# Feed-forward gate-up pairs of four feature tiles at a time, tokens stationary and 512 weight columns moving

## The chip, the cores and the metric

The kernel runs on one core of one Trainium2 chip. The metric is the device time of one execution in microseconds (us). Engines: TensorE (PE, its weight loads PEld), VectorE (DVE), ScalarE (ACT), GpSimd (POOL) and SyncE (SP), which here only issues transfers. By 0.2% of the time, 2.7 us, two versions can just be told apart.

## The reference

One decoder layer for 512 tokens of width 1024, in float32: a feed-forward half-step, a token mixing of three branches, and a second feed-forward half-step. The change touches the two feed-forward steps only:

```python
D_MODEL, SEQ, D_FF = 1024, 512, 2816
def rmsnorm(x, w):
    return x * lax.rsqrt(jnp.mean(x * x, axis=-1, keepdims=True) + EPS) * w
def swiglu(x, w_gu, w_down):
    g, u = jnp.split(x @ w_gu, 2, axis=-1)       # w_gu: 1024 x 5632
    return (jax.nn.silu(g) * u) @ w_down         # w_down: 2816 x 1024
h = h + 0.5 * rmsnorm(swiglu(rmsnorm(h, pre), w_gu, w_down), post)
...  # token mixing with its own norms and weights
h = h + 0.5 * rmsnorm(swiglu(rmsnorm(h, pre2), w_gu2, w_down2), post2)
```

## The kernel before

**Precision.** Every float32 operand is kept as a high part and a low part, both of type fp32r. The high part is a ScalarE copy (L173), the low part is the float32 value minus the high part, on VectorE (L168). One product of two tiles is three matmuls: high × high, high × low, low × high.

**The pairs.** D_FF = 2816 is 22 feature tiles of 128. Features 0 and 1 of each layer are computed plainly ("heads"). For each of the other 20, gate columns and up columns of `w_gu` are computed together, as a Strassen-Winograd scheme: contraction halves × (gate, up) against token halves, 7 products in place of 8. The operands of the tokens (`xop`) are made once per layer: `xhi`, `xlo` and t1 to t4 are the seven token-side sums. The weight-side sums are made per feature tile: four quarters of 512 × 128 are loaded, s1 or s3 (which of them depends on the place in the layer) are made by an accumulating transfer that POOL issues (L334), and the others by VectorE additions (`sum<-sum,st`). `product()` then holds a 128×128 weight tile stationary and moves 256 tokens: 12 matmuls of 128x256 (L399 to L401), 84 per pair. The outputs come with features on partitions, which is the layout the down projection needs as its stationary operand.

**The downs.** `down()` computes, for a token tile t and an output half hf, the contribution of a chunk of features: tokens stationary, 512 output columns moving, 3 matmuls per feature (L381, `px<-s,s`). The downs of a chunk (its size is in `CHUNKS1` and `CHUNKS2`) are issued between the pairs of the next chunk, and the last chunk's downs form the tail of the layer, with residual and post norm.

**Order and queues.** Each engine executes its own list in the order fixed when the program is built; a small planner (`tick`, the latencies `LAT`) decides in what order spawned parts are written. SP issues nearly all loads. POOL makes the rstd of the norms (L195) and issues the accumulating transfers. In the names of the trace `w` is a split weight (18 units, `NW`), `sum` a weight sum or quarter (5, `NSUM`), `st` a staged load (4, `NST`), `sh` a half-size staged load, `s` a 128×512 slot, `px` the PSUM bank of a down, `ps` other PSUM banks, `r` and `v` the rstd and its input.

Of the kernel before, what the change touches and what calls it, by code (L numbers as in the profile page):

```python
# [8 lines left out]
F32 = mybir.dt.float32  # L9
F32R = mybir.dt.float32r  # L10
# [7 lines left out]
P = 128  # L18
# [25 lines left out]
CHUNKS1 = (2, 4, 4, 4, 2, 6)  # L44
CHUNKS2 = (2, 4, 4, 4, 4, 4)

LAT = dict(comb=1.0, mem0=3.5, mem1=8.0, mem2=1.5, mem3=2.0, rest=1.0, hg=1.5, hgx=6.0, hg1=6.0, hg2=11.0, hg3=6.0, hg4=6.0, dil0=4.0, exp=2.0, dil1=9.0, dil2=5.0,
           dil3=3.0, norm=8.0, mnorm=5.0, mload=10.0, start=0.1, step=2.0, keep=2.0)
PLAN = dict(early1=2, plain1=2, early2=2, plain2=2)
# [3 lines left out]
class Layer:  # L53
# [89 lines left out]
    def fetch(self, out, in_):  # L143

        ins = self.tc.keep_in_program_order(self.nc.sync.dma_start(out=out, in_=in_))
        if self.strict:
            self.anchor = ins.ins
# [437 lines left out]
    def ffn(self, w_gu, w_down, w_post, ready, reload, after, chunks, early, plain, last=False):  # L585
# [5 lines left out]
        gw = self.col_tiles(w_gu, 0, plain)  # L591
        uw = self.col_tiles(w_gu, DFF, plain)
        pairs = self.pairs([(w_gu, f * P, DFF + f * P) for f in range(plain, NF)], lambda i: ("s1", "s3")[i < 4:])

        def swiglu(sg, su, act):
            nc.scalar.activation(sg, sg, AF.Silu)
            self.tt(sg, sg, su, ALU.mult)
            self.split(act[0], act[1], sg)

        def gu(ops, act):  # L600
            a, u, c, d, v = self.pair(ops)
            sg, su = self.slot(), self.slot()
            nc.scalar.copy(sg[:, :HT], a)
            self.tt(sg[:, HT:], u, c, ALU.add)
            self.tt(su[:, :HT], d, u, ALU.subtract)
            self.tt(su[:, HT:], v, u, ALU.subtract)
            swiglu(sg, su, act)
# [55 lines left out]
        f0, before, ws = 0, None, []  # L663
        for n in chunks:
            act = []
            for j in range(n):
                if before and 2 * j % n == 0:
                    ws = []
                    for i in range(0, before[1], 2):
                        ws += down_weights(before[0] + i, 2 * j // n)  # L670
                if f0 + j < early:
                    act.append(heads[f0 + j][1])
                else:
                    act.append(new_act())
                    if f0 + j < plain:
                        gu_plain([self.wcol(next(g)) for g in (gw, uw)], act[-1], slice(0, T))
                    else:
                        gu(begun or next(pairs), act[-1])
                        begun = None
                if before:  # L680
                    for i in range(8 * j // n, 8 * (j + 1) // n):
                        down(i % NT, i // NT, before[2], ws, before[0] == 0)
            before = (f0, n, act)
            f0 += n
# [603 lines left out]
def layer_kernel(ctx, tc, a, nbias, hmask, out):  # L1288
# [59 lines left out]
    def store(h, t):  # L1348
        for c, n in ((0, 512), (512, 256), (768, 256)) if t == NT - 1 else ((0, 512), (512, 512)):
# [5 lines left out]
                  reload(lambda t, hf: x[t * P:(t + 1) * P, HALVES[hf]]), follow(h1, a["mix_pre_w"][0]), CHUNKS1, PLAN['early1'], PLAN['plain1'])  # L1355
    z = L.mixing(a, ready, nbias)
    ready = L.out_proj(z, a["w_out"][0], a["mix_post_w"][0], reload(lambda t, hf: h1[t][hf]), follow(h2, a["ffn2_pre_w"][0]))
    L.ffn(a["ffn2_w_gu"][0], a["ffn2_w_down"][0], a["ffn2_post_w"][0], [lambda: ready[:2], lambda: ready[2:]], reload(lambda t, hf: h2[t][hf]), store, CHUNKS2, PLAN['early2'], PLAN['plain2'], True)
# [42 lines left out]
```

## Time and profile before

| | |
|---|---|
| median of 3 runs | 1341.71 us (1339.46 to 1341.76) |
| profiled execution | 1339.9 us, span 1338.1 us, granted TensorE clock 0.999 |
| PE busy | 1325.7 us, 9228 instructions |
| DVE, ACT, POOL busy | 1043.0, 753.9 and 87.3 us |
| transfers | 183.14 MB, mean 137 GB/s |

The first feed-forward layer fills about 0 to 433 us, the mixing 433 to 943, the second feed-forward layer 943 to 1338. Busy time says how long an engine had an instruction in work; matmuls overlap in the pipeline, so their pace is read from the starts of one after another. In a group's row the numbers are: total busy time, mean ns of one, the idle time of the engine before them, and what ended most of it.

### The profile page before, as it was taken

The numbers are of one execution on the slowest core, as the hardware profiler recorded it, in microseconds if no ns is written. First come the engines' busy times: TensorE is split into PE (matmuls) and PEld (weight loads), VectorE is DVE, ScalarE is ACT, GpSimd is POOL, SyncE is SP. The second block draws the span as 40 slices with busy tenths as digits, with TensorE's granted clock in tenths as the row PEclk, the third lists the DMA queues.
The fourth block names the chain that finished last, engine by engine and source line by source line (L and its number), as shares of the span: only waits on it lengthen the run. The fifth ranks groups of instructions, "written<-read, shape, count | busy, mean of one in ns | idle before, by whom it ended". The sixth has DMA issues, their size and how long they took to land.

```text
span 1338.1 us, 24335 instructions
## 1 busy us (share of the span) xinstructions
PE 1325.7 (99%) x9228; PEld 1234.3 (92%) x9228; DVE 1043.0 (78%) x1979; ACT 753.9 (56%) x1557; POOL 87.3 (7%) x116
## 2 busy tenths in 40 slices
PE   9999999999999999999999999999999999999997
PEld 8999999999898988899899999999899999999996
DVE  7987777687897975699769968888488877777765
ACT  7764544465566764455765755566366644445541
POOL 1011110110100000000000000000011111111100
PEclk9999999999999999999999999999999999999999
DMA  9587556565425335434223423334536766556523
GB/s 252 153 191 172 144 147 165 126 160 191 161 65 157 111 98 175 122 106 125 65 79 112 119 80 95 103 106 150 193 111 161 187 162 153 143 142 154 146 64 126
DMA packets 238611, 183.14 MB, mean 137 GB/s; under 512 B 11129, under 2 KB 200990, under 8 KB 238494
## 3 DMA queue, kind: packets, MB, share of 16 engines
q1 hardware_dynamic: 223702, 159.49, 39.6%
q0 software_dynamic: 10368, 18.88, 8.6%
q10 hardware_dynamic: 4424, 3.22, 0.8%
q8 instruction: 72, 1.18, 0.4%
q14 instruction: 45, 0.37, 0.1%
HBM read 153.21 MB, written 9.47 MB: 122 GB/s over the span
## 4 chain that ended last, share of the span: by engine, by line
PE 64%; DVE 2%; DMA 1%; ACT 0%; issue 0%; POOLq 0%; DVEq 0%; ACTq 0%
PE ps L381 16%; PE ps L399 12%; PE ps L400 12%; PE ps L401 12%; PE px L381 7%; PE px L386 4%; PE px L390 1%; DVE w L168 1%; DMA st<-in_ffn_w_gu_dram 0%; DVE s L168 0%; DMA sh<-in_w_in_dram 0%; DMA st<-in_w_out_dram 0%; DVE s L736 0%; ACT w L173 0%; DVE st L996 0%
## 5 line engine op out<-in xcount | busy, mean ns | idle before, releaser
L173 ACT ACTIVATE w<-sum 128x512 fp32r<-128x512 f32 x288 | 180.3, 631 | 210.4 <-PE ps L400 183.4
L168 DVE TENSOR_TENSOR w<-sum,w 128x512 fp32r<-128x512 f32 x288 | 196.8, 687 | 72.8 <-ACT w L173 71.8
L399 PE MATMUL ps<-xhi,w 128*128 128x256 f32 x864 | 244.7, 283 | 0.1
L400 PE MATMUL ps<-xlo,w 128*128 128x256 f32 x864 | 244.5, 283 | 0.0
L401 PE MATMUL ps<-xhi,w 128*128 128x256 f32 x864 | 244.5, 283 | 0.0
L173 ACT ACTIVATE w<-st 128x512 fp32r<-128x512 f32 x240 | 150.1, 630 | 116.2 <-PE ps L400 84.0
L168 DVE TENSOR_TENSOR w<-st,w 128x512 fp32r<-128x512 f32 x248 | 168.5, 687 | 32.1 <-ACT w L173 29.4
L381 PE MATMUL px<-s,s 128*128 128x512 f32 x816 | 193.0, 390 | 0.0
L168 DVE TENSOR_TENSOR s<-s,s 128x256 f32<-128x256 f32 (+3 forms) x317 | 176.4, 562 | 14.9 <-ACT s L173 3.9
L381 PEld LDWEIGHTS px<-s,s 128*128 128x128 f32 x816 | 150.6, 188 | 29.9 <-DVE s L168 0.4
L399 PEld LDWEIGHTS ps<-xhi,w 128*128 128x128 f32 x864 | 165.5, 192 | 2.5 <-ACT s L408 0.5
L400 PEld LDWEIGHTS ps<-xlo,w 128*128 128x128 f32 x864 | 165.5, 192 | 2.0
L401 PEld LDWEIGHTS ps<-xhi,w 128*128 128x128 f32 x864 | 165.5, 192 | 0.0
L168 DVE TENSOR_TENSOR sum<-sum,st 128x512 f32<-128x512 f32 x176 | 120.3, 685 | 7.1 <-issue 3.9
L168 DVE TENSOR_TENSOR s<-s,ps 128x256 f32<-128x256 f32 (+1 forms) x195 | 93.0, 477 | 29.2 <-PE ps L381 22.1
L399 PE MATMUL ps<-t3hi,w 128*128 128x256 f32 x288 | 83.6, 290 | 0.0
L168 DVE TENSOR_TENSOR s<-s,px 128x512 f32<-128x512 f32 x73 | 49.8, 683 | 43.0 <-PE px L381 34.8
L399 PE MATMUL ps<-t4hi,w 128*128 128x256 f32 x288 | 82.1, 285 | 0.0
L399 PE MATMUL ps<-t1hi,w 128*128 128x256 f32 x288 | 82.0, 285 | 0.0
L401 PE MATMUL ps<-t2hi,w 128*128 128x256 f32 x288 | 81.7, 284 | 0.0
L401 PE MATMUL ps<-t3hi,w 128*128 128x256 f32 x288 | 81.7, 284 | 0.0
L399 PE MATMUL ps<-t2hi,w 128*128 128x256 f32 x288 | 81.6, 283 | 0.0
(198 smaller groups left out, 2996.6 us busy)
## 6 DMA issues: line engine op xcount, KB each, us to landing
st<-in_ffn_w_gu_dram SPq DMA_DIRECT2D x48, 512.0 KB, 5.0
st<-in_w_in_dram SPq DMA_DIRECT2D x48, 512.0 KB, 3.8
st<-in_ffn_w_down_dram SPq DMA_DIRECT2D x44, 512.0 KB, 4.0
sum<-in_ffn_w_gu_dram SPq DMA_DIRECT2D x80, 256.0 KB, 3.4
sh<-in_ffn_w_gu_dram SPq DMA_DIRECT2D x40, 256.0 KB, 3.3
sum<-st POOLq DMA_DIRECT2D x40, 256.0 KB, 3.3
sum<-sh POOLq DMA_DIRECT2D x32, 256.0 KB, 3.6
sum<-in_w_in_dram SPq DMA_DIRECT2D x32, 256.0 KB, 2.9
```

Source lines behind the costliest of these rows:

```text
L168: ins = self.nc.vector.tensor_tensor(out=out, in0=a, in1=b, op=op)
L173: self.pin(self.nc.scalar.activation(hi, src, AF.Copy))
L381: self.pin_pe(mm(out, lhsT=lhs[l], rhs=rhs[r], start=a, stop=b))
L386: self.nc.tensor.matmul(out, lhsT=lhsT, rhs=rhs, start=start, stop=stop, **k)
L390: self.pin_pe(self.nc.tensor.transpose(out, in_, self.ident))
L399: mm(out, lhsT=lh, rhs=rh, start=first and k == 0, stop=False, skip_group_check=True)
L400: mm(out, lhsT=lh, rhs=rl, start=False, stop=False, skip_group_check=True)
L401: mm(out, lhsT=ll, rhs=rh, start=False, stop=k == 3, skip_group_check=True)
```

## The change

Four feature tiles are computed together. Now the token operand is stationary (128 tokens) and 512 weight columns, four features wide, move: `wide_product()` has 2 token tiles × 4 contraction tiles × 3 = 24 matmuls of 128x512 (L637 to L639 of the changed kernel), 7 products per group, five groups per layer, in the order 1, 6, 2, 5, 7, 4, 3. Weights are loaded in rows of 512 columns (2 KB). Both s1 and s3 (raw 5 and 7) come from a load and an accumulating transfer out of memory (`both()`, L598); raw 6 and raw 3 are VectorE additions.

The outputs have tokens on partitions, so they are turned (`turn()`): VectorE transposes 32×32 blocks (L698, STREAM_TRANSPOSE), SP writes the result to memory (L701, `turn<-s`) and reads it back with the blocks in place (L704, `s<-turn`), then ScalarE and VectorE make high and low part. The table `DOWNS` says how many downs of the group before follow each product. Down weights are loaded one feature at a time through `st2` (two buffers, `sh`). At the end of the first layer two features are kept back, so its tail has six features; the second layer's has four.

```diff
-CHUNKS1 = (2, 4, 4, 4, 2, 6)
-CHUNKS2 = (2, 4, 4, 4, 4, 4)
+DOWNS = ((0, 1, 1, 1, 2, 1, 2), (0, 1, 1, 1, 1, 1, 1), (0, 1, 1, 1, 1, 0, 0))
-           dil3=3.0, norm=8.0, mnorm=5.0, mload=10.0, start=0.1, step=2.0, keep=2.0)
-PLAN = dict(early1=2, plain1=2, early2=2, plain2=2)
+           dil3=3.0, norm=8.0, mnorm=5.0, mload=10.0, start=0.1, step=2.0, keep=2.0, turn=5.0, back=4.0)
+EARLY = 2
...
+    def wide(self, w, c1, c2):
+        k0 = w.rearrange("(k p) c -> p k c", p=P)
+        raw, ops = {}, {}
+        def quarter(j, h, c):
+            raw[j] = [x[:, i, :] for x in (self.load(w, 4 * h + 2 * n, 2, c, 512) for n in range(2)) for i in range(2)]
+        def both(j, h1, d1, h2, d2):
+            raw[j] = []
+            for k in range(4):
+                u = self.wpool.tile([P, 512], F32, tag="sum", bufs=NSUM, name=f"sum{self.uid()}")
+                self.bring(u, k0[:, 4 * h1 + k, d1:d1 + 512])
+                self.nc.gpsimd.dma_start(out=u, in_=k0[:, 4 * h2 + k, d2:d2 + 512], accum_op=ALU.add)
+                raw[j].append(u)
+        def fetch(j):
+            if j == 1:
+                quarter(1, 0, c1)
+            elif j == 6:
+                both(5, 0, c2, 1, c2)
+            elif j == 2:
+                quarter(2, 1, c1)
+            elif j == 7:
+                both(7, 0, c2, 0, c1)
+            elif j == 4:
+                quarter(4, 1, c2)
+        def get(j):
+            with self.tc.issue_after(self.opened[0]), self.tc.issue_after(self.opened[1]):
+                return operand(j)
+        def operand(j):
+            if j == 6:
+                for k in range(4):
+                    self.tt(raw[1][k], raw[1][k], raw[5][k], ALU.add)
+                raw[6] = raw[1]
+            elif j == 3:
+                for k in range(4):
+                    self.tt(raw[2][k], raw[2][k], raw[6][k], ALU.add)
+                raw[3] = raw[2]
+            return [self.wsplit(raw[j][k]) for k in range(4)]
+        return fetch, get
+    def wide_product(self, banks, w, j, first=True):
+        x = self.xop[j]
+        mm = self.nc.tensor.matmul
+        for t in range(2):
+            ts = slice(t * P, (t + 1) * P)
+            for k in range(4):
+                lh, ll = x[0][:, k, ts], x[1][:, k, ts]
+                mm(banks[t], lhsT=lh, rhs=w[k][0], start=first and k == 0, stop=False, skip_group_check=True)
+                mm(banks[t], lhsT=lh, rhs=w[k][1], start=False, stop=False, skip_group_check=True)
+                mm(banks[t], lhsT=ll, rhs=w[k][0], start=False, stop=k == 3, skip_group_check=True)
+                self.tick(3 * 0.2268)
+    def wide_pair(self, ops, turned):
+        nc = self.nc
+        a = [self.psum() for _ in range(2)]
+        self.wide_product(a, ops(1), 1)
+        u = [self.slot() for _ in range(2)]
+        for i in range(2):
+            nc.scalar.copy(u[i], a[i])
+        yield
+        b = [self.psum() for _ in range(2)]
+        self.wide_product(b, ops(6), 6)
+        for i in range(2):
+            self.tt(u[i], u[i], b[i], ALU.add)
+        yield
+        self.wide_product(a, ops(2), 2, False)
+        g = [self.slot() for _ in range(2)]
+        for i in range(2):
+            nc.scalar.activation(g[i], a[i], AF.Silu)
+        yield
+        c = [self.psum() for _ in range(2)]
+        self.wide_product(c, ops(5), 5)
+        p5 = [self.slot() for _ in range(2)]
+        for i in range(2):
+            nc.scalar.copy(p5[i], c[i])
+        yield
+        d = [self.psum() for _ in range(2)]
+        self.wide_product(d, ops(7), 7)
+        v = [self.slot() for _ in range(2)]
+        for i in range(2):
+            nc.scalar.copy(v[i], d[i])
+        for i in range(2):
+            self.tt(v[i], v[i], p5[i], ALU.subtract)
+        yield
+        self.wide_product(d, ops(4), 4, False)
+        for i in range(2):
+            self.tt(v[i], v[i], u[i], ALU.subtract)
+        s = [self.slot() for _ in range(2)]
+        for i in range(2):
+            self.tt(s[i], d[i], u[i], ALU.subtract)
+            self.tt(g[i], g[i], s[i], ALU.mult)
+            turned[i] = self.spawn(self.turn(g[i], turned, i))
+        yield
+        self.wide_product(c, ops(3), 3, False)
+        for i in range(2):
+            g = self.slot()
+            self.tt(g, u[i], c[i], ALU.add)
+            nc.scalar.activation(g, g, AF.Silu)
+            self.tt(g, g, v[i], ALU.mult)
+            turned[2 + i] = self.spawn(self.turn(g, turned, 2 + i))
+        yield
+    def turn(self, g, turned, t):
+        blocks = self.slot()
+        self.nc.vector.transpose(blocks.rearrange("p (b f i) -> p f b i", b=4, f=4), g.rearrange("p (f j b) -> p f b j", f=4, b=4))
+        n = self.uid()
+        d = self.dram.tile([4, 32, 4, P], F32, tag=f"turn{n}", name=f"turn{n}")
+        self.nc.sync.dma_start(out=d.rearrange("a j b x -> (a j) (b x)"), in_=blocks)
+        yield LAT['turn']
+        swapped = self.slot()
+        self.nc.sync.dma_start(out=swapped.rearrange("p (a x) -> p a x", a=4), in_=d.rearrange("a j b x -> (j b) a x"))
+        yield LAT['back']
+        hi, lo = self.slot((P, 4, P), F32R), self.slot((P, 4, P), F32R)
+        four = lambda x: x.rearrange("p f (a i) -> p f a i", a=4)
+        src = swapped.rearrange("p (a f i) -> p f a i", a=4, f=4)
+        self.nc.scalar.activation(four(hi), src, AF.Copy)
+        self.tt(four(lo), src, four(hi).bitcast(F32), ALU.subtract)
+        turned[4 + t] = (hi, lo)
...
-        gw = self.col_tiles(w_gu, 0, plain)
-        uw = self.col_tiles(w_gu, DFF, plain)
-        pairs = self.pairs([(w_gu, f * P, DFF + f * P) for f in range(plain, NF)], lambda i: ("s1", "s3")[i < 4:])
...
+        gw = self.col_tiles(w_gu, 0, early)
+        uw = self.col_tiles(w_gu, DFF, early)
...
         def down_weights(f, hf):
-            st = self.load(w_down, f, 2, hf * 512, 512)
-            return [self.wsplit(st[:, j, :], slot=True) for j in range(2)]
+            st = self.stage.tile([P, 512], F32, tag="st2", bufs=2, name=f"sh{self.uid()}")
+            self.bring(st, w_down[f * P:(f + 1) * P, HALVES[hf]])
+            return self.wsplit(st, slot=True)
         def down(t, hf, act, ws, first, bank=self.paux, cs=slice(0, 512)):
             acc = bank((P, cs.stop - cs.start))
-            self.proj_N(acc, act, slice(t * P, (t + 1) * P), [(w[0][:, cs], w[1][:, cs]) for w in ws])
+            lhs = act(t)
+            for k in range(len(ws)):
+                self.mm3(acc, lhs[k], (ws[k][0][:, cs], ws[k][1][:, cs]), k == 0, k == len(ws) - 1)
             if first:
                 nc.scalar.copy(y[t][hf], acc)
             else:
                 self.tt(y[t][hf][:, cs], y[t][hf][:, cs], acc, ALU.add)
+        wides = [self.wide(w_gu, f * P, DFF + f * P) for f in range(early, NF, 4)]
+        todo = [(s, j) for s in range(len(wides)) for j in (1, 6, 2, 5, 7, 4, 3)]
+        fetched = 0
+        def operands(s):
+            def get(j):
+                nonlocal fetched
+                upto = todo.index((s, j)) + 4
+                while fetched < min(upto, len(todo)):
+                    n, i = todo[fetched]
+                    wides[n][0](i)
+                    fetched += 1
+                return wides[s][1](j)
+            return get
...
-        begun = None
+        turned = [None] * 8
+        pair = self.wide_pair(operands(0), turned)
         for i in range(2):
             if i == 1 and resumed:
-                begun = self.pair_begin(next(pairs))
+                next(pair)
             self.need(*tasks[i])
             for w, act in heads if i or resumed else ():
                 gu_plain(w, act, slice(i * HT, (i + 1) * HT))
...
+        cut = lambda x, t: x[:, t * P:(t + 1) * P]
+        def of_heads(t):
+            return [(cut(act[0], t), cut(act[1], t)) for w, act in heads]
+        def of_wide(turned, f0, f1):
+            def act(t):
+                self.need(turned[t])
+                return [(turned[4 + t][0][:, f, :], turned[4 + t][1][:, f, :]) for f in range(f0, f1)]
+            return act
+        def downs(f0, n, act):
+            for hf in range(2):
+                ws = [down_weights(f0 + f, hf) for f in range(n)]
+                for t in range(NT):
+                    yield
+                    down(t, hf, act, ws, f0 == 0)
+        tail = 0 if last else 2
+        f0, n, act = 0, early, of_heads
+        for s in range(len(wides)):
+            end = s == len(wides) - 1
+            if s:
+                turned = [None] * 8
+                pair = self.wide_pair(operands(s), turned)
+            behind = downs(f0, n - tail if end else n, act)
+            for j, m in enumerate(DOWNS[2 if end and tail else 1 if end else 0]):
+                if j or s or not resumed:
+                    next(pair, None)
+                for _ in range(m + (j == 0)):
+                    next(behind, None)
+            for _ in behind:
+                pass
+            if not end:
+                f0, n, act = f0 + n, 4, of_wide(turned, 0, 4)
+        held, ahead = act, of_wide(turned, 0, 4)
+        act = (lambda t: held(t)[4 - tail:] + ahead(t)) if tail else ahead
+        f0, n = f0 + n - tail, 4 + tail
         ws, spare = [], list(self.spare())
         for j in range(n):
-            st = self.load(w_down, before[0] + j, 1, 0, D)
+            st = self.load(w_down, f0 + j, 1, 0, D)
             ws.append([])
             for hf in range(2):
```

TensorE, at the boundary between two pairs or groups of the first layer. Before, the last matmuls of a down (px) and then a pair's first product (a weight tile w_ stationary, 256 tokens moving):

```order
L381 MATMUL px_1847<-s_1680,s_1117 128x512
L381 MATMUL px_1847<-s_1681,s_1117 128x512
L381 MATMUL px_1847<-s_1680,s_1118 128x512
L399 MATMUL ps_1873<-xhi_88,w_1875 128x256
L400 MATMUL ps_1873<-xlo_90,w_1875 128x256
L401 MATMUL ps_1873<-xhi_88,w_1876 128x256
L399 MATMUL ps_1873<-xhi_88,w_1875 128x256
```

After, the same place two products into a group (px_2397 is the group's first down, s_2321 to s_2334 the split down weights, s_2226 and s_2227 the turned activations of a token tile, w_2415 to w_2428 the split weights of product 2):

```order
L380 MATMUL px_2397<-s_2321,s_2227 128x512
L637 MATMUL ps_2259<-w_2415,xhi_89 128x512
L638 MATMUL ps_2259<-w_2416,xhi_89 128x512
L639 MATMUL ps_2259<-w_2415,xlo_91 128x512
L637 MATMUL ps_2259<-w_2419,xhi_89 128x512
L638 MATMUL ps_2259<-w_2420,xhi_89 128x512
L380 MATMUL px_2397<-s_2327,s_2226 128x512
L639 MATMUL ps_2259<-w_2419,xlo_91 128x512
L637 MATMUL ps_2259<-w_2423,xhi_89 128x512
L638 MATMUL ps_2259<-w_2424,xhi_89 128x512
L639 MATMUL ps_2259<-w_2423,xlo_91 128x512
L380 MATMUL px_2397<-s_2328,s_2226 128x512
```

Where a down was finished before a product began, the first down of a group is now written in between the matmuls of product 2.

POOL, in the opening of the first layer (`r` are the rstds of the four token tiles, then the first accumulating transfers). Before:

```order
L195 TENSOR_TENSOR r_183<-v_182,mhalf 128x1
L195 TENSOR_TENSOR r_195<-v_194,mhalf 128x1
L195 TENSOR_TENSOR r_266<-v_265,mhalf 128x1
L195 TENSOR_TENSOR r_325<-v_324,mhalf 128x1
L334 DMA sum_611<-st_605 128x512
L334 DMA sum_620<-st_614 128x512
```

After:

```order
L194 TENSOR_TENSOR r_183<-v_182,mhalf 128x1
L194 TENSOR_TENSOR r_195<-v_194,mhalf 128x1
L194 TENSOR_TENSOR r_266<-v_265,mhalf 128x1
L598 DMA sum_599<-in_ffn_w_gu_dram 128x512
L598 DMA sum_602<-in_ffn_w_gu_dram 128x512
L194 TENSOR_TENSOR r_325<-v_324,mhalf 128x1
L598 DMA sum_605<-in_ffn_w_gu_dram 128x512
L598 DMA sum_608<-in_ffn_w_gu_dram 128x512
```

The fourth rstd, r_325, now stands behind two accumulating transfers.

VectorE, at the boundary between two groups of the first layer. Before, a stretch between two pairs:

```order
L168 TENSOR_TENSOR s_2213<-ps_2145,s_2104 128x256
L168 TENSOR_TENSOR s_2212<-s_2212,s_2213 128x512
L168 TENSOR_TENSOR w_2485<-sum_2481,w_2484 128x512
L168 TENSOR_TENSOR s_2074<-s_2212,s_2073 128x512
L168 TENSOR_TENSOR s_116<-s_116,px_2222 128x512
L168 TENSOR_TENSOR s_118<-s_118,px_2236 128x512
L168 TENSOR_TENSOR w_2503<-sum_2256,w_2502 128x512
L168 TENSOR_TENSOR sum_2480<-sum_2481,st_2252 128x512
L168 TENSOR_TENSOR s_2281<-s_2263,ps_2282 128x256
L168 TENSOR_TENSOR w_2521<-sum_2259,w_2520 128x512
```

After, around the end of a group (s_2254 and s_2256 are turned results read back, ps_2337 the result of the next group's product 6, sh_ are down weights, st_2151 a raw quarter):

```order
L698 STREAM_TRANSPOSE s_2215<-s_2211 128x4x4x32
L167 TENSOR_TENSOR s_123<-s_123,px_2241 128x512
L167 TENSOR_TENSOR s_2227<-s_2187,s_2226 128x512
L167 TENSOR_TENSOR s_2231<-s_2189,s_2230 128x512
L167 TENSOR_TENSOR w_2420<-st_2151,w_2419 128x512
L167 TENSOR_TENSOR w_2424<-st_2153,w_2423 128x512
L167 TENSOR_TENSOR s_2296<-s_2254,s_2295 128x512
L167 TENSOR_TENSOR w_2428<-st_2153,w_2427 128x512
L167 TENSOR_TENSOR s_2300<-s_2256,s_2299 128x512
L167 TENSOR_TENSOR w_2476<-sum_2069,w_2475 128x512
L167 TENSOR_TENSOR st_2151<-st_2151,st_1967 128x512
L167 TENSOR_TENSOR st_2153<-st_2153,st_1969 128x512
```

The low parts of the turned results (s_2227, s_2231, s_2296, s_2300) stand between the low parts of the next group's weights (w_).

SP, at the same boundary, after:

```order
L701 DMA turn_2135<-s_2133 128x512
L704 DMA s_2189<-turn_2135 128x4x128
L701 DMA turn_2209<-s_2207 128x512
L701 DMA turn_2217<-s_2215 128x512
L704 DMA s_2254<-turn_2209 128x4x128
L704 DMA s_2256<-turn_2217 128x4x128
L154 DMA sum_2342<-in_ffn_w_gu_dram 128x512
L154 DMA st_2411<-in_ffn_w_gu_dram 128x2x512
L154 DMA sh_2325<-in_ffn_w_down_dram 128x512
L154 DMA sh_2331<-in_ffn_w_down_dram 128x512
```

Before, loads alone stood there:

```order
L155 DMA sum_1690<-in_ffn_w_gu_dram 128x4x128
L155 DMA st_1674<-in_ffn_w_down_dram 128x2x512
L155 DMA st_1686<-in_ffn_w_gu_dram 128x8x128
L155 DMA sum_1693<-in_ffn_w_gu_dram 128x4x128
L155 DMA sh_1688<-in_ffn_w_gu_dram 128x4x128
L155 DMA sum_1867<-in_ffn_w_gu_dram 128x4x128
L155 DMA sum_1870<-in_ffn_w_gu_dram 128x4x128
```

The loads of the next group (sum_2342, st_2411) and the later down weights (sh_2325, sh_2331) now come behind the turned writes and reads on SP.

More of the change, by code (lines that the diff above doesn't have):

```diff
@@ L583, in open @@
         self.spawn(rest(2)), self.spawn(rest(3))
-    def ffn(self, w_gu, w_down, w_post, ready, reload, after, chunks, early, plain, last=False):
+    def wide(self, w, c1, c2):
[35 more added lines that the diff above has]
+        return fetch, get
@@ L588, in ffn @@
+    def ffn(self, w_gu, w_down, w_post, ready, reload, after, early, last=False):
         nc = self.nc
@@ L590, in ffn @@
         y = [[self.slot() for _ in range(2)] for _ in range(NT)]
-        gw = self.col_tiles(w_gu, 0, plain)
-        uw = self.col_tiles(w_gu, DFF, plain)
-        pairs = self.pairs([(w_gu, f * P, DFF + f * P) for f in range(plain, NF)], lambda i: ("s1", "s3")[i < 4:])
[L595 to L607, printed above, removed]
+        gw = self.col_tiles(w_gu, 0, early)
+        uw = self.col_tiles(w_gu, DFF, early)
         def gu_mm(w, cs):
@@ L662, in ffn @@
                 gu_plain(w, act, slice(i * HT, (i + 1) * HT))
[L663 to L684, printed above, removed]
+        cut = lambda x, t: x[:, t * P:(t + 1) * P]
@@ L1354, in layer_kernel @@
     ready = L.ffn(a["ffn1_w_gu"][0], a["ffn1_w_down"][0], a["ffn1_post_w"][0], Source,
-                  reload(lambda t, hf: x[t * P:(t + 1) * P, HALVES[hf]]), follow(h1, a["mix_pre_w"][0]), CHUNKS1, PLAN['early1'], PLAN['plain1'])
+                  reload(lambda t, hf: x[t * P:(t + 1) * P, HALVES[hf]]), follow(h1, a["mix_pre_w"][0]), EARLY)
     z = L.mixing(a, ready, nbias)
     ready = L.out_proj(z, a["w_out"][0], a["mix_post_w"][0], reload(lambda t, hf: h1[t][hf]), follow(h2, a["ffn2_pre_w"][0]))
-    L.ffn(a["ffn2_w_gu"][0], a["ffn2_w_down"][0], a["ffn2_post_w"][0], [lambda: ready[:2], lambda: ready[2:]], reload(lambda t, hf: h2[t][hf]), store, CHUNKS2, PLAN['early2'], PLAN['plain2'], True)
+    L.ffn(a["ffn2_w_gu"][0], a["ffn2_w_down"][0], a["ffn2_post_w"][0], [lambda: ready[:2], lambda: ready[2:]], reload(lambda t, hf: h2[t][hf]), store, EARLY, True)
 def constants():
```

## The prediction

> **What bounds the kernel now.** I read the page's busy shares first, then the costliest groups, the windows, and last the chain of waits inside one feed-forward layer.
>
> ```profile
> PE 1325.7 (99%) x9228; PEld 1234.3 (92%) x9228; DVE 1043.0 (78%) x1979; ACT 753.9 (56%) x1557; POOL 87.3 (7%) x116
> PEclk9999999999999999999999999999999999999999
> L399 PE MATMUL ps<-xhi,w 128*128 128x256 f32 x864 | 244.7, 283 | 0.1
> L400 PE MATMUL ps<-xlo,w 128*128 128x256 f32 x864 | 244.5, 283 | 0.0
> L381 PE MATMUL px<-s,s 128*128 128x512 f32 x816 | 193.0, 390 | 0.0
> ...
> 20.00:424.00 404.00, 403.87 (x2789) 377.38 (x2789) 323.56 (x581) 230.99 (x459) 38.02 (x47) 1.00 0.60 157
> 1000.00:1300.00 300.00, 300.00 (x2136) 283.66 (x2136) 229.20 (x404) 161.67 (x317) 29.40 (x34) 1.00 0.57 145
> 1100.00:1140.00 40.00, 40.00 (x271) 37.12 (x271) 28.02 (x50) 18.65 (x36) 5.16 (x6) 1.00 0.58 142
> ```
>
> The last three are windows: length, then busy time and count of PE, PEld, DVE, ACT and POOL, the clock, the DMA share, GB/s. In both feed-forward layers TensorE is busy to within 0.13 us in 404, at clock 1.00; VectorE has 28.02 of 40 us, ScalarE 18.65, DMA 0.58. So what these layers take is the number of matmuls times their spacing. A group's mean (283, 390 ns) is latency and overlaps; spacing must come from the chain and the timeline.
>
> ```profile
> 1085.77 5.47 PE px L381 x24
> 1101.31 5.47 PE px L381 x24
> ...
> 1308.63 1.52 PE L381 MATMUL ps<-w,s 128*128 128x512 f32 x6
> 1311.35 1.52 PE L381 MATMUL ps<-w,s 128*128 128x512 f32 x6
> ```
>
> Between the two px pieces lies one pair of 84 narrow (256-column) matmuls: 1101.31 − 1085.77 − 5.47 = 10.07 us, 119.9 ns each. Twelve wide (512-column) ones lie between the last two starts: 2.72 us, 226.7 ns. The 24 of a px piece give 227.9 with the change of shape. Two narrow cost 239.8, one wide 226.7: each merged pair saves 13.1 ns.
>
> **The change part by part.**
>
> *The stream.* 40 pairs of 84 narrow matmuls go, 3360 in all; ten groups of 7 × 24 = 168 wide ones come, 1680. Saved: 3360 × 0.1199 − 1680 × 0.2267 = 402.9 − 380.9 = 22.0 us. With 0.2279 it is 20.0; I take 22.0, because in a 24-matmul product the change of shape is no part of the pace. All of it is on the path, since TensorE never waits there.
>
> The Trainium skill, "TensorE: Matmul & The Clock Gate", section "Wait — 56ns, not 53.3ns?", gives a warm spacing of N ÷ 2.4 GHz plus about 2.5 ns. By that one merged pair saves 2.5 ns, and 1680 of them 4.2 us where the sum has 22.0. This trace's 119.9 and 226.7 ns hold about 13 ns beyond columns ÷ 2.4 GHz, so here the measurement decides.
>
> *Vector work.* How a strided read is priced:
>
> ```profile
> 598.45 0.42 DVE L168 TENSOR_TENSOR s<-s,s 128x256 f32<-128x256 f32 x1
> 598.79 0.68 DVE L168 TENSOR_TENSOR sum<-sum,st 128x512 f32<-128x512 f32 x1
> 599.39 0.62 DVE L168 TENSOR_TENSOR s<-s,s 128x256 f32<-128x256 f32 x1
> 599.92 0.68 DVE L168 TENSOR_TENSOR w<-sh,w 128x512 fp32r<-128x512 f32 x1
> 600.52 0.62 DVE L168 TENSOR_TENSOR s<-s,ps 128x256 f32<-128x256 f32 x1
> ```
>
> Start to start, a 512-wide operation takes 0.60, a dense 256-wide one 0.34, and a 256-wide one that reads every fourth element 0.53: 0.20 us more for 256 elements. The trace has no 32×32 transpose. The new one reads 512 elements with a stride of four: estimate 0.60 + 2 × 0.20 = 1.0 us; ends 0.6 (dense) and 1.4 (the stride charged twice). Per four features VectorE had 60 × 0.60 + 20 × 0.34 = 42.8 us in four times 15.54 = 62.2, and gets 70 × 0.60 + 4 × 1.0 = 46.0 in about 60. With 1.4 it is 47.6. Free time of 12 us hides it on average, so 0, except where a wait stands in VectorE's order (the boundary, below). ScalarE gains four 512-wide hi copies per group and loses the smaller PSUM copies: 0, hidden by its 53% idle. PSUM, two banks per product in place of one half bank: 0, as a bank is read for less time than the product after it takes.
>
> *Transfers.*
>
> ```profile
> st<-in_ffn_w_gu_dram SPq DMA_DIRECT2D x48, 512.0 KB, 5.0
> sum<-in_ffn_w_gu_dram SPq DMA_DIRECT2D x80, 256.0 KB, 3.4
> sum<-st POOLq DMA_DIRECT2D x40, 256.0 KB, 3.3
> h<-s SPq DMA_DIRECT2D x16, 256.0 KB, 2.0
> s<-h SPq DMA_DIRECT2D x16, 256.0 KB, 5.0
> s<-v SPq DMA_DIRECT2D x12, 256.0 KB, 3.8
> s<-in_ffn_post_w_dram SPq DMA_DIRECT2D x4, 256.0 KB, 5.2
> ```
>
> KB each and median us to landing. Per four features come 4 writes and 4 reads of 256 KB, 2.1 MB over 60 us, 35 GB/s beside 142: the DMA share 0.58 would go to 0.58 × 177 / 142 = 0.72. The accumulates, 80 for 72, now read memory where they read SBUF; as transfers they are in the 0.58 already. The packets of the gate-up weights become 2 KB where they were 512 B, which this trace doesn't price. With 0.28 left free I take 0 in the steady part.
>
> *The opening of the first layer.* POOL's fourth rstd (r_325) is moved behind two accumulates that each wait for a plain load.
>
> ```profile
> 14.99 0.55 POOL L195 TENSOR_TENSOR r<-v,mhalf 128x1 f32<-128x1 f32 x1 [6.94 <-DVE v L192]
> 19.26 0.55 POOL L195 TENSOR_TENSOR r<-v,mhalf 128x1 f32<-128x1 f32 x1 [3.72 <-DVE v L192]
> 23.74 1.03 POOL L334 DMA_DIRECT2D sum<-st  x1 [3.93 <-DMA sum<-in_ffn_w_gu_dram]
> ...
> 15.83 2.09 SPq L155 DMA_DIRECT2D sum<-in_ffn_w_gu_dram  x2
> 19.84 1.42 DVE L500 SCALAR_TENSOR_TENSOR s<-s,r,s 128x512 f32<-128x512 f32 x2 [0.66 <-POOL r L195]
> 21.51 0.60 PE L390 MATMUL px<-ident,s 128*128 128x128 f32 x4
> ...
> 13.00:40.00 27.00, 26.90 (x218) 26.14 (x217) 24.32 (x45) 19.56 (x43) 3.00 (x4) 1.00 0.70 185
> ```
>
> That rstd now runs at 19.26, VectorE scales with it at 19.84, TensorE turns the result at 21.51: 0.66 + 0.25 = 0.9 us of slack. If the loads land 3.4 us after 15.83 and the two accumulates take 0.9 each, rstd starts at 21.1, 1.8 late, and TensorE loses 0.9. If the first accumulate goes only at 23.74 as it does now, rstd is at 25.8, 6.5 late; with VectorE's backlog (24.32 of 27 us busy there) eating the slack, TensorE loses 6.5. I take 3.5, about the middle, for neither row is nearer.
>
> *The eight boundaries between groups* (four per layer). Count from E, the end of a group's last product. Two downs of 12 matmuls follow (to E + 5.4), product 1 (to 10.9), product 6 (to 16.3), then the next group's first down beside product 2, which wants the low half of the third down weight (s_2328) after 16 matmuls, E + 19.9. VectorE's order: its first turned tile may start at E − 2.7, when the product's first bank is done; by 0.60 per operation and 1.0 per transpose the last transpose ends at E + 5.5. SP writes it (2.0), reads it back (3.8 to 5.0), ScalarE makes the high part (0.6): E + 11.9 to 13.1, while VectorE has reached that low part (s_2300) at 10.1 and waits 1.8 to 3.0. Then twelve operations until s_2328 is done: E + 19.7 to 20.9 against 19.9. Behind the same wait on SP stand the loads of st_2411, sh_2325 and sh_2331: issued from about E + 8, landed 3.4 to 5.0 later, in time. So −0.2 to 1.0, and with 1.4 us per transpose and slower landings up to 3.0. I take 0.9: 8 × 0.9 = 7.2, ends 0 and 24.
>
> *The end of the first layer.* The eight reloads of x and the two gains stand on SP behind the last turned read.
>
> ```profile
> 943.07 6.11 SPq L145 DMA_DIRECT2D s<-h  x8
> L168 DVE TENSOR_TENSOR s<-s,s 128x512 f32<-128x512 f32 x103 | 69.6, 687 | 5.4 <-DMA s<-in_ffn_post_w_dram 1.1 <-ACT s L596 0.5
> ```
>
> At 0.76 us an issue (6.11 / 8) from E + 7.5, the last gain is issued at E + 15 and lands 5.2 later, E + 20; if the 2.1 MB of mixing weights ahead of it and its own 2.6 MB must go first at 142 GB/s, 33 us, it is there at E + 40. TensorE wants the first transposes of the next stage about 134 wide matmuls after E, 30.4 us. VectorE waits 1.1 us for such a gain already. I take 2, ends 0 and 4 (later than that, the loads stop competing).
>
> *The start of the second layer.* Product 1 needs four 512-wide splits before its last matmuls, where one 512-wide tile held all of it: 3 × 0.60 = 1.8 us more. Half is hidden by the plain matmuls beside it: 1, ends 0 and 2.
>
> The sum: −22.0 + 3.5 + 7.2 + 2 + 1 = −8.3. The profiled execution took 1339.9 (span 1338.1 and 1.8 around it), so 1331.6; the median of the runs, 1341.71, lies 1.8 above it: 1333.4. I say 1333.
>
> **Rivals.** (A) *Everything but the stream is hidden.* Order is fixed at build time, and loads were early before: TensorE waits 0.00 us in 300. Against it, the row at 23.74. Gives 1341.71 − 22.0 to −18.5, 1320 to 1323.
>
> (B) *The trip to memory decides*: at each boundary VectorE stands waiting for the read-back with the next group's weight splits behind it. Other stalls are 6.5, so the gain is gone at (22.0 − 6.5) / 8 = 1.9 us each; 2.3 makes it slower beyond doubt; 3.0 gives −22.0 + 24 + 6.5 = +8.5, 1350. For it: reads of 5.0 us, VectorE at 77% with waits in its order. Against: four products lie between a turned result and its first use.
>
> (C) *Merging saves almost nothing,* for instance because wide matmuls with a fresh 512-column moving tile run at up to twice the narrow spacing, 0.2398. Then the 13.7 of stalls stands alone: 1355. Against it, 24 downs in 5.47 us, which read such fresh tiles. Ending near here is what the skill's section named above would give, 1351 with 4.2 saved; the trace speaks against it.
>
> (D) *Half-way*: boundaries of 1.6 to 2.3 leave the time within what a measurement tells from no change, 0.2% or 2.7 us.
>
> **How the numbers follow.** My forecast 0.57 (its own range 1326 to 1339: boundaries of 0.1 to 1.5), A 0.20, B 0.10, C 0.03, D 0.10. Faster A and the forecast, 0.77; same D, 0.10; slower B and C, 0.13. The range runs from A's low end, 1319, to the middle of B, 1346, and leaves out C and the outer half of B.
>
> **What will show it.** Wide product matmuls, 1680 of them, start 0.227 apart; if not, C. A gap in TensorE between 21 and 28 us before the transposes of token tile 3, with POOL's rstd behind two accumulates; if none, that 3.5 is wrong. VectorE's waits on the read-back, near 2 to 3 us a boundary, and TensorE gaps of about 1 us some 18 to 20 us after each group's end; none means A, above 2 means B. Transposes near 1.0 us each. At the first layer's end a wait on the gain or on x. What would make all this wrong is a cost spread through the stream: a DMA share near 1 with weights late in the middle of groups, or VectorE above 90%.

## The result, and the profile after

The changed kernel takes 1377.18 us (median of four, 1372.76 to 1378.53) against 1340.59: a ratio of 1.0268, interval 1.024 to 1.0297. It is 37 us slower where the forecast was 8 us faster, and lies above the range (1319 to 1346). The profiled execution took 1378.38 us, span 1376.6, 38.5 more than the span before.

The page, two of its groups, the two long windows taken of the kernel before, and two rows of TensorE's timeline in the first group:

```profile
PE 1324.1 (96%) x7548; PEld 1146.9 (83%) x7548; DVE 1053.1 (76%) x1911; ACT 728.1 (53%) x1457; POOL 94.8 (7%) x124
PEclk9999999999999999999999999999999999999998
L380 PE MATMUL px<-s,s 128*128 128x512 f32 x816 | 210.2, 397 | 24.0 <-ACT s L172 22.8
L172 ACT ACTIVATE s<-sh 128x512 fp32r<-128x512 f32 x68 | 42.8, 632 | 57.5 <-DMA sh<-in_ffn_w_down_dram 57.5
...
20.00:424.00 404.00, 379.96 (x1749) 309.35 (x1748) 305.77 (x503) 197.64 (x373) 41.96 (x52) 0.98 0.60 172
1000.00:1300.00 300.00, 289.64 (x1359) 237.97 (x1358) 230.50 (x369) 151.64 (x278) 31.23 (x37) 1.00 0.61 169
...
60.42 0.39 PE L638 MATMUL ps<-w,xhi 128*128 128x512 f32 x1
61.10 0.39 PE L638 MATMUL ps<-w,xhi 128*128 128x512 f32 x1
```

The wide products run as forecast: three of them from 60.42 to 61.10, 0.227 each. But TensorE, gapless before, now stands still for 24 of the 404 us and 10 of the 300, although VectorE has more idle time than in the 20:424 window of before and the mean DMA share is the same 0.60 (in the 1000:1300 window 0.61 for 0.57). A mean share says nothing of lateness. The down matmuls (`px`) carry the wait: 22.8 us until ScalarE has made the high part of a down weight (s, from the landing buffer sh), and ScalarE in turn waited 57.5 us for the loads of sh.

To place the loss I summed, over all neighbouring matmuls, start-to-start time less the pace of the shape (0.2267, 0.1199, 0.1095 us for 512, 256, 128 columns). The groups end with the last wide product, the end is the 80 us behind it, and the second layer begins with its first wide product. In us, for the profiled executions:

| stretch | before | after | e1 | e5 | e6 | e9 |
|---|---|---|---|---|---|---|
| opening (to 42 us) | 6.3 | 12.1 | 13.0 | 8.1 | 6.7 | 6.6 |
| first layer: groups | 2.5 with its end | 25.6 | 10.1 | 6.8 | 2.8 | 2.6 |
| first layer: its end | (above) | 9.7 | 7.4 | 9.0 | 8.1 | 5.9 |
| second layer | 0.9 | 15.8 | 4.0 | 4.4 | 4.1 | 4.1 |

With 14.3 − 10.8 in the mixing stage, that is 57 us of loss more than before; the span needs 38.5 + 22.0 = 60.5, so 3.5 us are not placed.

How one stall arises, from the chain of waits between 120 and 150 us, SP's timeline there and one row of VectorE's (start, length, what):

```profile
120.84 6.51 DMA sum<-in_ffn_w_gu_dram
128.82 4.92 DMA sum<-in_ffn_w_gu_dram
134.84 0.55 POOL s L1228
135.40 2.66 DMA s<-in_b_gate_dram
138.06 1.29 DVE s L167 x2
139.37 7.19 DMA sh<-in_ffn_w_down_dram
146.64 0.64 ACT s L172
147.32 0.80 PE px L380
...
116.62 1.45 SPq L154 DMA_DIRECT2D sh<-in_ffn_w_down_dram  x2
118.16 10.98 SPq L154 DMA_DIRECT2D sum<-in_ffn_w_gu_dram  x5
130.62 0.38 SPq L154 DMA_DIRECT2D st<-in_ffn_w_gu_dram  x1
136.51 2.02 SPq L154 DMA_DIRECT2D st<-in_ffn_w_gu_dram  x3
139.37 9.61 SPq L154 DMA_DIRECT2D sh<-in_ffn_w_down_dram  x4
...
138.65 0.69 DVE L167 TENSOR_TENSOR s<-sh,s 128x512 fp32r<-128x512 f32 x1
```

At 116.62 SP issues two down weights of a half, which fill both landing buffers. Behind them stand five loads into `sum` buffers; a product by s1 or s3 takes four of the five there are, so these go out one by one as VectorE's splits free them. SP then stands until 135.40 at a small load whose tile POOL clears only behind its accumulating transfers. Only at 139.37, after the next raw weights too, does the third down weight go, and TensorE stands from 143.2 to 147.32. But what released that load is not the queue: its landing buffer still held the first down weight, which VectorE finished splitting at 139.34.

The same holds nearly throughout. TensorE's 22.8 us are 17 waits; for 16 of them, 19.5 us, the down weight's load was issued 0.03 us after VectorE's split had freed its landing buffer. It then took 3 to 7 us to land. The 17th, 3.3 us just after 80, is another: that down weight had been loaded from 50.81 on, but ScalarE takes it behind a raw weight (w from st), and the raw weight's load stood on SP behind five `sum` loads. TensorE's waits, SP's timeline and ScalarE's:

```profile
PE px L380 <- ACT s L172: 22.8, 17, 4.1
...
61.79 12.63 SPq L154 DMA_DIRECT2D sum<-in_ffn_w_gu_dram  x5
75.31 5.74 SPq L154 DMA_DIRECT2D st<-in_ffn_w_gu_dram  x4
81.94 0.63 ACT L172 ACTIVATE w<-st 128x512 fp32r<-128x512 f32 x1 [2.50 <-DMA st<-in_ffn_w_gu_dram]
82.94 1.15 ACT L172 ACTIVATE s<-sh 128x512 fp32r<-128x512 f32 x2
```

The stall costs more than its length. TensorE's timeline and the windows behind it:

```profile
147.32 0.80 PE L380 MATMUL px<-s,s 128*128 128x512 f32 x1 [4.14 <-ACT s L172]
...
144.00:146.00 2.00, 0.00 (x0) 0.00 (x0) 0.00 (x0) 0.00 (x0) 0.00 (x0) 0.92 0.50 193
148.00:150.00 2.00, 2.00 (x6) 1.58 (x5) 0.62 (x1) 0.00 (x0) 0.00 (x0) 0.50 0.43 141
150.00:152.00 2.00, 2.00 (x6) 1.56 (x5) 0.43 (x1) 0.00 (x0) 0.00 (x0) 0.50 0.37 121
152.00:154.00 2.00, 2.00 (x9) 1.59 (x9) 1.42 (x3) 1.17 (x2) 0.00 (x0) 0.87 0.00 0
```

For about 5 us after the gap the granted clock is 0.50, six matmuls in 2 us. About 3.4 us of half clock follow the gaps of 3.7 us at 22 and 3.5 us at 80, and a cluster of shorter ones near 355. Over windows of 4 us, busy time × (1 − clock) sums to 6.9 us; before, it is 0. The Trainium skill, "TensorE: Matmul & The Clock Gate", section "What's actually happening", has the clock at half after an idle window of about 3.4 us; the three gaps of 3.5 to 4.3 us agree, while near 355 no gap was over 1.7 us.

### The profile page after: what moved, and what is told of

It is laid out like the page before. It is cut to its first block, busy times and chain, and to the rows that moved or that the text cites. A ratio compares the mean times of both kernels' runs of the same rounds, so it can differ in the third digit from the quotient of the medians.

```text
span 1376.6 us, 21006 instructions
## 1 busy us (share of the span) xinstructions
PE 1324.1 (96%) x7548; PEld 1146.9 (83%) x7548; DVE 1053.1 (76%) x1911; ACT 728.1 (53%) x1457; POOL 94.8 (7%) x124
## 4 chain that ended last, share of the span: by engine, by line
PE 58%; DVE 17%; DMA 15%; ACT 4%; issue 3%; POOL 1%; SPq 0%; POOLq 0%; DVEq 0%; ACTq 0%
PE ps L380 14%; PE ps L398 7%; PE ps L399 6%; PE ps L400 6%; PE px L380 6%; DVE s L167 6%; DVE w L167 4%; DMA sh<-in_ffn_w_down_dram 4%; PE ps L638 4%; PE ps L637 4%; PE ps L639 4%; PE px L385 4%; DMA sum<-in_ffn_w_gu_dram 3%; DVE s L698 2%; PE px L389 2%
## 5 line engine op out<-in xcount | busy, mean ns | idle before, releaser
L167 DVE TENSOR_TENSOR w<-st,w 128x512 fp32r<-128x512 f32 x368 | 245.4, 686 | 24.3 <-ACT w L172 21.4
L380 PE MATMUL px<-s,s 128*128 128x512 f32 x816 | 210.2, 397 | 24.0 <-ACT s L172 22.8
L167 DVE TENSOR_TENSOR s<-s,s 128x512 f32<-128x512 f32 (+3 forms) x277 | 169.5, 621 | 29.8 <-ACT s L672 17.4
L598 POOL DMA_DIRECT2D sum<-in_ffn_w_gu_dram x80 | 70.4, 949 | 876.8 <-DVE w L167 438.5
L398 PE MATMUL ps<-xhi,w 128*128 128x256 f32 x384 | 108.9, 284 | 0.0
L400 PE MATMUL ps<-xhi,w 128*128 128x256 f32 x384 | 108.7, 283 | 0.0
L399 PE MATMUL ps<-xlo,w 128*128 128x256 f32 x384 | 108.6, 283 | 0.0
L638 PE MATMUL ps<-w,xhi 128*128 128x512 f32 x240 | 93.9, 391 | 0.6 <-DVE w L167 0.6
L637 PE MATMUL ps<-w,xhi 128*128 128x512 f32 x240 | 93.5, 391 | 0.4 <-ACT w L172 0.4
L639 PE MATMUL ps<-w,xlo 128*128 128x512 f32 x240 | 93.5, 390 | 0.0
L380 PE MATMUL ps<-s,w 128*128 128x512 f32 (+1 forms) x384 | 80.2, 364 | 0.0
L380 PE MATMUL ps<-w,xhi 128*128 128x512 f32 x256 | 80.0, 393 | 0.0
L398 PEld LDWEIGHTS ps<-xhi,w 128*128 128x128 f32 x384 | 73.6, 192 | 0.7 <-ACT s L407 0.2
L399 PEld LDWEIGHTS ps<-xlo,w 128*128 128x128 f32 x384 | 73.6, 192 | 0.6
L400 PEld LDWEIGHTS ps<-xhi,w 128*128 128x128 f32 x384 | 73.6, 192 | 0.0
L172 ACT ACTIVATE s<-sh 128x512 fp32r<-128x512 f32 x68 | 42.8, 632 | 57.5 <-DMA sh<-in_ffn_w_down_dram 57.5
```

The source lines that it names most:

```text
L167: ins = self.nc.vector.tensor_tensor(out=out, in0=a, in1=b, op=op)
L172: self.pin(self.nc.scalar.activation(hi, src, AF.Copy))
L380: self.pin_pe(mm(out, lhsT=lhs[l], rhs=rhs[r], start=a, stop=b))
L398: mm(out, lhsT=lh, rhs=rh, start=first and k == 0, stop=False, skip_group_check=True)
L399: mm(out, lhsT=lh, rhs=rl, start=False, stop=False, skip_group_check=True)
L400: mm(out, lhsT=ll, rhs=rh, start=False, stop=k == 3, skip_group_check=True)
```

## Experiments

Theory Q: down weights come late because their loads queue on SP behind loads that wait for `sum` buffers, with two landing buffers to run ahead in. Its two halves, the queue and the buffers, are parted by e1, e3 and the issue times above. Rivals: T, the turned results' trip through memory; D, the traffic itself. Ratios are to the kernel before, run beside each.

**e1, landing buffers alone.**

```diff
-NSLOT = 37
+NSLOT = 35
-  tag="st2", bufs=2
+  tag="st2", bufs=4
```

> Four landing buffers for the down weights (sh) in place of two, paid for with two 128x512 slots (35 for 37); nothing else. Theory Q (the down weights come late because their loads stand on SP behind weight loads that wait for a free sum buffer, and only two of a half's four can be on their way): TensorE's 22.8 us of waiting for the high part of a down weight fall below 8, the time comes to 1350 to 1360. Theory T (the trip of the turned results through memory holds VectorE and SP): no change beyond 3 us, 1373 to 1379. Theory D (the transfers themselves fill the engines in bursts): no change beyond 3 us.

1346.21 us, ratio 1.0041 (1.0025 to 1.0058): 31 us of the 37 lost came back, more than Q expected, by two buffers. TensorE's waits and windows in e1:

```profile
PE px L380 <- ACT s L172: 3.3, 1, 3.3
...
20.00:424.00 404.00, 390.56 (x1892) 325.77 (x1892) 321.16 (x534) 210.33 (x398) 41.87 (x52) 0.99 0.63 181
1000.00:1300.00 300.00, 298.79 (x1388) 247.63 (x1387) 234.85 (x377) 152.91 (x279) 31.03 (x36) 1.00 0.61 173
```

22.8 us in 17 waits became 3.3 in one, the wait just after 80 us; all 16 waits on a landing buffer are gone. The bytes and the trip are the same and the DMA share is no lower, so neither T nor D can be the main cause.

**e2, no trip.** High and low part straight from the transposed blocks; the write, the read and the placing are left out.

```diff
-        self.nc.sync.dma_start(out=d.rearrange(...), in_=blocks)
-        self.nc.sync.dma_start(out=swapped.rearrange(...), in_=d.rearrange(...))
+        swapped = blocks
```

> The turned results are not written to memory and read back; high and low part are made straight from the transposed blocks, so the activations are not in their place in the output. Transposes, splits and downs stay. Theory T: nearly all stalls of the two feed-forward layers go, 1340 to 1352. Theory Q: only the wait of the loads behind the turned reads goes, one of the two late pairs of down weights per group gets better: 1360 to 1372. Theory D: 21 MB fewer of 206, less than 8 us.

1361.97 us, 1.0162 (1.0139 to 1.0184), within what Q expected: 15 us less, and 15.6 us of TensorE's wait for down weights stayed. In the first layer's groups the loss falls from 25.6 to 17.9, at its end from 9.7 to 5.0; in the second layer it stays (15.4 for 15.8). The down weights that TensorE waits for are still issued 0.03 us after their landing buffer is freed.

**e3, sum buffers alone.**

```diff
-NSLOT = 37
-NSUM = 5
+NSLOT = 34
+NSUM = 8
```

> Eight sum buffers in place of five, paid for with three slots (34 for 37). Theory Q: SP no longer stands at the sums of the next product, and the loads behind them go out earlier: 1350 to 1365. Theory T and theory D: no change beyond 3 us; if loads bunch even more, D gives a few us slower.

1358.86 us, 1.0131 (1.011 to 1.0152): 18 us less, as Q expected; 14.2 us of waiting for down weights stayed. The wait just after 80 us is gone; the 15 that stay are all on a landing buffer. By the loss sums the groups of the first layer lose 12.3 here and 10.1 in e1, for 25.6, and the second layer 13.8 here and 4.0 in e1, for 15.8. So the block by the sums matters in the first layer, where curing either hides some of the other; in the second layer nearly all is the landing buffers.

**e4, the order on POOL.**

```diff
+        self.last_r = self.nc.gpsimd.tensor_tensor(out=r, ...).ins     # in rstd()
+                with self.tc.issue_after(self.last_r):
                     self.nc.gpsimd.dma_start(out=u, ..., accum_op=ALU.add)
```

> The first accumulating transfers are ordered behind the fourth rstd on POOL, as the kernel before had it; nothing else. All theories: the gap of 3.7 us near 22 us and the half clock behind it (about 2 us) go, 3 to 6 us less: 1371 to 1374. If the gap stays, the rstd was not its cause.

1369.11 us, 1.0214 (1.0198 to 1.0229), 8 us less, more than the 3 to 6 expected. POOL's timeline, first of the changed kernel, then of e4:

```profile
15.73 0.55 POOL L194 TENSOR_TENSOR r<-v,mhalf 128x1 f32<-128x1 f32 x1 [6.94 <-DVE v L191]
22.45 1.95 POOL L598 DMA_DIRECT2D sum<-in_ffn_w_gu_dram  x2 [6.18 <-DMA sum<-in_ffn_w_gu_dram]
23.75 1.23 POOL L194 TENSOR_TENSOR r<-v,mhalf 128x1 f32<-128x1 f32 x1
```

```profile
20.63 0.55 POOL L194 TENSOR_TENSOR r<-v,mhalf 128x1 f32<-128x1 f32 x1 [3.72 <-DVE v L191]
22.90 3.75 POOL L599 DMA_DIRECT2D sum<-in_ffn_w_gu_dram  x4 [1.72 <-DMA sum<-in_ffn_w_gu_dram]
```

The rstd that waited behind two accumulates until 23.75 runs at 20.63, and no gap is left near 22 us. By the sum of losses the opening gives 3.9 of the 8; the rest is spread over the later stretches, and I have no run that says why. With intervals of some 4 us for the changed kernel's time and 2 us for this one, 8 is not clearly more than 3 to 6.

**e5, e1 and e4 together.** 

> Four landing buffers for the down weights and the fourth rstd ahead of the accumulating transfers, together (35 slots). If the two stalls are separate: 1346.2 - 8 = 1338, within 0.3% of the kernel before. If one of the two only hid behind the other's loads, 1342 to 1346.

1339.96 us, 0.9995 (0.9986 to 1.0003): the two stalls add, 6 us less than e1, and the change has come back to the time of before.

**e6, e5 with eight sums** (NSLOT 32, NSUM 8). 

> The same with eight sum buffers for five (32 slots for 35). Theory Q: what is left of the stalls in the first layer's first two groups goes too, 1328 to 1334, clearly below the kernel before. Rival: three fewer slots now hold up the turned results or the down weights, which cost one of each: 1338 to 1348.

1335.26 us, 0.9961 (0.995 to 0.9973), 1 us above Q's expectation. The groups of the first layer lose 2.8 us in place of 6.8, no slot shortage shows. This beats the kernel before.

**e7, the order of asking alone**, buffers as in the changed kernel.

```diff
+                if j == 0:
+                    next(behind, None)        # asks for the first half's down weights
                 if j or s or not resumed:
                     next(pair, None)
-                for _ in range(m + (j == 0)):
+                for _ in range(m):
```

> Only the order: a group's first four down weights are asked for ahead of its first product, so that their loads stand ahead of the next raw weights on SP; two landing buffers and five sums as in the changed kernel. Theory Q with order as the cause: one of the two late pairs of a group goes, 1358 to 1368. If the number of buffers is the cause (the third load waits for the split of the first whatever the order): 1372 to 1379.

1362.7 us, 1.0155 (1.0132 to 1.0178): 14 us less, about half of what the buffers bring. The first half's loads are in time; the second half's are not (a gap of 4.2 us at 139.4, 3.4 at 1119.8), and there the third load is still issued 0.03 us after the first one's split. Order is part of the cause; the run moves SP's loads and the splits on ScalarE and VectorE together, so it does not say which order.

**e8, e5 without the trip** (left out as in e2). 

> e5 without the trip of the turned results through memory (the activations are not in their place). It prices the trip where the down weights come in time. My forecast's 0.9 us per boundary would make it 7 us faster than e5, 1331; if the trip is hidden, within 3 us of e5.

1332.09 us, 0.9942 (0.9927 to 0.9956): 8 us less than e5, so the trip, with its 21 MB and one slot per turned result, does cost what I had put down for it, but not where. At the end of the first layer the loss falls from 9.0 to 4.6; in the second layer from 4.4 to 3.2; in the first layer's groups it does not fall (6.8 and 7.9).

**e9, e6 with the gains ahead of the reloads.**

```diff
-        h = reload()
         gain = self.bcast_gain(w_post)
+        h = reload()
```

> e6 (four landing buffers, eight sums, rstd first) with the two post gain loads of a feed-forward layer ahead of the eight reloads on SP. At the first layer's end the chain of e6 runs through a reload of x and then a gain (10.4 us), and TensorE loses 8.1 us there against 2.5 before. If the gain's place in the queue is the cause: 3 to 5 us less than e6, 1330 to 1332. If the bytes (2.6 MB) or the turned reads ahead of them are: within 2 us of e6.

1331.15 us, 0.9922 (0.9909 to 0.9934), 4 us less than e6: at the first layer's end the place in the queue counted. This is the best version. Its page and windows:

```profile
PE 1308.3 (99%) x7548; PEld 1143.5 (86%) x7548; DVE 1056.6 (80%) x1911; ACT 730.2 (55%) x1457; POOL 95.0 (7%) x124
20.00:424.00 404.00, 399.55 (x1962) 334.32 (x1961) 334.56 (x554) 220.87 (x413) 41.82 (x51) 1.00 0.64 188
1000.00:1300.00 300.00, 299.21 (x1347) 246.67 (x1346) 235.49 (x372) 148.49 (x266) 27.87 (x32) 1.00 0.61 173
```

TensorE works 399.55 of the 404 us and 299.21 of the 300, at a higher DMA share (0.64 in the first window) and with VectorE busier than in the kernel before (334.56 for 323.56).

**e10, e9 with the reloads on ScalarE's queue** (`nc.scalar.dma_start` for `fetch` in `reload`). 

> e9 with the eight reloads issued by ScalarE in place of SP, so that they do not stand behind the last turned reads. If the turned reads ahead of them on SP are what is late (e8 without the trip had 4.4 us less loss at this place than e5): 2 to 4 us less than e9. If ScalarE then stands at its issues for free slots and delays the splits: slower than e9.

1333.21 us, 0.9933 (0.992 to 0.9947): not faster than e9, the interval overlaps. Moving the reloads off SP does not help; the end of the layer loses 8.5 us in this profile against 5.9.

**e11, no accumulating transfers.** Each sum keeps its first term only; the POOL transfer is left out.

```diff
-                self.nc.gpsimd.dma_start(out=u, in_=k0[...], accum_op=ALU.add)
```

> The changed kernel without the accumulating transfers: the sums keep their first term only, so the feed-forward results are not the layer's; 80 transfers of 256 KB, 21 of 206 MB, are left out, and the sums are complete 6.5 us earlier. Theory D (bursts fill the engines) and theory Q agree on a gain, not on its size: by D, 10% fewer bytes bring 4 to 8 us; by Q the sums free their buffers earlier and SP moves on, 15 us or more, 1362 or below.

1349.94 us, 1.006 (1.0045 to 1.0074): 27 us less, the size that Q expected and beyond D's 4 to 8. The run drops bytes and lateness together, so by itself it does not part the two; e1, with all the bytes, does.

**e12, the kernel before with the gains first.** 

> The kernel before with the two post gain loads ahead of the reloads, as in e9. It tells how much of e9's gain belongs to that edit alone: TensorE loses 2.5 us at the first layer's end in the kernel before, so at most 2.5 us, 1338.5 to 1341; if it were 4 us as between e6 and e9, the wide products would deserve only 6 us of the 10.

1339.76 us, 0.9995 (0.9986 to 1.0004): nothing. In the kernel before, where TensorE lost at most 2.5 us at this place, e9's edit is worth nothing; that its worth comes from the turned reads pushing the gain back is argued, not shown.

## Why the prediction was wrong

- *The stream, −22.0.* Right: wide products at 0.227 us, and with the stalls cut to e9's the kernel is 10 us faster than before. Rival C is out.
- *Transfers, "0 in the steady part".* This step failed, and it carries most of the miss. I added bytes to a DMA share and left out which free buffer each load waits for. Two landing buffers serve the four down weights of a half, so the third can be loaded only when the first has been split, shortly before it is wanted itself; and four 512-column sums per product come out of five buffers. The groups of the first layer lose 25.6 us and the second layer 15.8, where e1 leaves 10.1 and 4.0. The landing times I took from before were low as well, probably because the loads now go out in bursts (last point below). The page's issue rows (KB each, us to landing):

```profile
sum<-in_ffn_w_gu_dram SPq DMA_DIRECT2D x80, 256.0 KB, 5.3
sum<-in_ffn_w_gu_dram POOLq DMA_DIRECT2D x80, 256.0 KB, 6.5
turn<-s SPq DMA_DIRECT2D x40, 256.0 KB, 2.1
s<-turn SPq DMA_DIRECT2D x40, 256.0 KB, 2.8
```

  A sum took 3.4 + 3.3 before and takes 5.3 + 6.5 now.
- *The boundaries, +7.2, and rival B.* The place was right, the mechanism was not. I had the loads of the later down weights issued from about E + 8, "in time", and VectorE standing for the read-back. TensorE's wait at the boundary is for those loads: at the group that ends at E = 163.2 the third down weight's load goes at 179.52, E + 16.3, when its landing buffer comes free. Beside product 2 of the eight groups these waits add up to 7.9 us, so that 7.2 came near by luck; beside product 4, where the sum had nothing, come 11.5 more. The read-back comes in 2.8 us, earlier than the 3.8 to 5.0 I used:

```profile
L709 ACT ACTIVATE s<-s 128x512 fp32r<-128x512 f32 x40 | 24.3, 624 | 9.6 <-DMA s<-turn 9.6
L698 DVE STREAM_TRANSPOSE s<-s 128x512 f32<-128x512 f32 x40 | 43.4, 1085 | 0.3
DVE s L167 <- ACT s L709: 2.6, 9, 0.4
```

  ScalarE waits 9.6 us in all for 40 of them. VectorE waits 2.6 us in nine times, 0.4 at most, for the high parts made of them, where I had 1.8 to 3.0 at each boundary and rival B as much or more; B is out. The transposes are 1.085 us each, near the estimate of 1.0. Of the 8 us between e5 and e8, the part that the loss sums place lies at the layer's end.
- *The opening, +3.5.* The mechanism was right: rstd at 23.75, between my 21.1 and 25.8. TensorE's gap was 3.7 us; 3.5 was the middle of 0.9 and 6.5, so its closeness is partly luck. With the half clock, which was not in the sum, the loss table has 5.8; e4's time has 8, and that difference is open.
- *The end of the first layer, +2 (0 to 4).* Right mechanism, mis-sized: 9.7 against at most 2.5 before, so at least 7.2. The chain of waits of the changed kernel there:

```profile
355.81 3.85 DMA turn<-s
360.09 0.50 SPq L144
360.63 4.97 DMA s<-in_x_dram
365.66 5.97 DMA s<-in_ffn_post_w_dram
```

  x and then the gain, one after the other behind the last turned read. I let the two overlap, and took the competing loads as a reason for a bound and not for delay.
- *The second layer's start, +1.* Two gaps of 0.57 and 0.79 us near 1030, 1.4 in all: right.
- *Half clock after a gap.* Not in the sum at all; 6.9 us. The Trainium skill's page named above has the rule, and I weighed only its spacing formula.
- *Signs named beforehand.* "A DMA share near 1 with weights late in the middle of groups" was written as what would make all of it wrong. The mean share stayed at 0.60; in windows of 20 us of the first layer it went from 0.13 (40 to 60 us) to 1.00 (120 to 140).

## What to carry to other kernels

When a change makes the unit of work four times as wide, count for every pool how many units one step now holds against the buffers there are. For a load that comes late, find what released it: here it was mostly the split that freed its own buffer, and once the in-order queue, with a load in front that waited for another buffer. The mean DMA share shows neither. Bytes over time is the last check, not the first. A stall of a few us on TensorE is to be priced with the half clock that follows it, and two buffers can be worth more than the whole change.

## What the runs showed of the hardware

Gaps of 3.5 to 4.3 us on TensorE were followed by 3.4 to 5 us at a granted clock of 0.50 (matmuls of 512 columns 0.43 us apart); single gaps up to 2.1 us in the second layer were not. Near 355 the clock fell although no gap was over 1.7 us: from 352 to 358 TensorE was busy 3.65 of 6 us. An accumulating transfer from memory took 6.5 us to land where one from SBUF had taken 3.3, though loads of the same size rose as well, so how much of it is the source is open.
